# First layer's input projection weights in buffers of their own, loaded once and kept for both chains

## The chip, the cores and the metric

The kernel runs on one core of a Trainium2 chip. The metric is the device time of one execution in microseconds (us): the median of several runs, and beside it the time of the one execution that the profiler recorded. The engines are TensorE (PE in the rows; its weight loads are PEld), VectorE (DVE), ScalarE (ACT), GpSimd (POOL) and SyncE (SP, which only issues transfers). Transfers issued by SP, ACT and POOL run on 16 shared DMA engines.

## What is computed

Two layers of a backbone that runs two groups of tokens through the same weights: 128 context tokens (one block, `b = 0`) and 256 latent tokens (two blocks, `b = 1, 2`). Cut to what matters here:

```
for l in range(2):
    mod = silu(cond) @ w_mod[l] + b_mod[l]          # 6 vectors of 1024; sh1, sc1, g1, sh2, sc2, g2
    h   = LN(x) * (1 + sc1) + sh1
    proj = h @ w_in[l]                              # 1024 x 1696, for context AND latent tokens
    mix = concat(gqa(proj), mla(proj), gmlp(proj)) @ w_o[l]
    x   = LN(alpha * x + g1 * mix)
    h2  = LN(x) * (1 + sc2) + sh2
    q   = h2 @ peer_wq[l];  ids, g = top-k of the product keys of q
    x   = LN(alpha * x + g2 * sum_k g_k * gelu(u[ids_k] . h2) * v[ids_k])   # PEER, 16384 experts
```

The latent tokens attend to cached context keys, not to the context chain's own result, so within a layer the two chains are independent. `w_in[l]` (6.95 MB in float32) is needed by both.

## The kernel before, in words

Each layer has a first stage (projection, attention, output projection of both chains, then the product-key queries of the context) and a second stage (PEER). In PEER the latent tokens go densely over all experts on TensorE, while for the 128 context tokens VectorE works on rows that GpSimd gathers (`gt`, four buffers, 256 gathers a layer: `u_step` and `v_step`). The gathers can start when the context's `ids` are written.

A scheduler decides the order on each engine, from the order in which the code is emitted, from priorities (`hp()` lifts the context chain, `crit()` lifts it further) and from its own timing; each engine then runs its list in order. Large weights come through a ring of six 512 KB buffers (`ring`, `RB = 6`), all issued by SP: a piece's load waits on SP until the piece six places earlier has been used, and everything behind it in SP's list waits too. In the first layer the ring serves `wm` (pieces of `w_mod`, eight to one of the six vectors; `wm_1`, `wm_0` are scale and shift, without which no projection can start), `wic` and `wil` (14 pieces of `w_in` for context and latents, the same data, loaded once for each chain by `project`), `woc`/`wol` (pieces of `w_o`), `wq` (query weights) and later the expert tables.

`project` makes `hT` (normalised, modulated, transposed input), then takes the 14 pieces in turn: eight matmuls per token block into a PSUM bank (`psic` context, `psil` latents), copied out by ScalarE to `proj`. The string `ORD` says in which order the first layer's parts are emitted: `p` the context projection, `2 4 3` three vectors of `w_mod`, `a` attention and `o` output projection of the context, each `l` one piece of the latents' projection. After it come `ctx_picks` (context queries `psqp`, scores `pssk`, `top_list`, `routing` to `ids`), what is left of the latents' projection, five vectors of the second layer's `w_mod`, the latents' attention (`pssl` scores, `psT` transposes, `pso` values) and their output projection (`psol`), then the sixth vector of the first layer. PSUM tag `m` has one bank, shared by `psm` (the sums of `w_mod`), `psc` (their transposes) and the context scores.

Of the kernel before, what the change touches and what calls it, by code (L numbers as in the profile page):

```python
# [8 lines left out]
F32 = mybir.dt.float32  # L9
# [36 lines left out]
def tile_fn(ctx: ExitStack, tc, A, outs):  # L46
    nc = tc.nc
# [5 lines left out]
    def pool(es, name, bufs=1, **kw):  # L53
        return es.enter_context(tc.tile_pool(name=name, bufs=bufs, reuse_waits="tile", **kw))
# [9 lines left out]
    def psum(es, spec):  # L64

        for tag, n in spec.items():
            banks[tag] = pool(es, f"ps_{tag}", n, space=PSUM)

    def pS(tag, name):
        return banks[tag].tile([128, 512], F32, name=name, tag=tag)  # L70

    def run(g, n=None):

        for k, _ in enumerate(g):
            if n is not None and k + 1 == n:
                return

    def hp():
        return tc.high_priority(offset=HP) if HP else ExitStack()

    def crit(on=True):
        return tc.high_priority(offset=2 * HP) if CRIT and on else ExitStack()
# [71 lines left out]
    def load(src, name, n=1024, cring=None):  # L154

        t = ring.tile([128, 1024], F32, name=name, tag="ring") if cring is None else             cring.tile([128, 1024], F32, name=name, tag="cring", bufs=2)
        nc.sync.dma_start(t[:, :n], src)
        return t[:, :n]
# [34 lines left out]
    def transposed_mod(b, l, ks, kh, dst4, name, XP, tag):  # L193

        r = 0 if b == 0 else 1
        xh = XP.tile([128, D], F32, name=name + "xh", tag="xh")
        normalise(xh, x[b], *ln_stats(x[b], name, "clk"[b], xh if b in AL1 else None))
        for h in range(2):
            ps = pS(tag, name + "pst")
            for c in range(4):  # L200
                T.transpose(ps[:, c * 128:(c + 1) * 128], xh[:, (h * 4 + c) * 128:(h * 4 + c + 1) * 128], ident)
            d = dst4(h)
            for c in range(4):
                cc = h * 4 + c
                sc, sh = cols[l][:, ks, cc, r:r + 1], cols[l][:, kh, cc, r:r + 1]
                if c % 2:
                    V.tensor_scalar(d[:, c, :], ps[:, c * 128:(c + 1) * 128], sc, sh, op0=OP.mult, op1=OP.add)
                else:
                    hmark.append(S.activation(d[:, c, :], ps[:, c * 128:(c + 1) * 128], AF.Identity, bias=sh,
                                              scale=sc))  # L210
        return xh
# [35 lines left out]
    def project(l, ch):  # L247

        ch.hT = {b: ch.P.tile([128, 8, 128], F32, name=f"hT{b}", tag=f"hT{i}") for i, b in enumerate(ch.bs)}
        for b in ch.bs:  # L250
            with crit(b):
                transposed_mod(b, l, 1, 0, lambda h: ch.hT[b][:, h * 4:h * 4 + 4, :], "m1", ch.P, ch.tT)
        ch.proj = {b: ch.P.tile([128, IN_W], F32, name=f"proj{b}", tag=f"proj{i}") for i, b in enumerate(ch.bs)}
        for j in range(14):
            w0 = j * 128
            n = min(128, IN_W - w0)
            wv = load(A["w_in"][l, :, w0 * 8:(w0 + n) * 8], f"wi{ch.g}{j}", n * 8, ch.cring)
            wv = wv.rearrange("p (c n) -> p c n", c=8)
            for b in ch.bs:
                ps = pS(ch.tS, "psi" + ch.g)  # L260
                for c in range(8):
                    T.matmul(ps[:, :n], lhsT=ch.hT[b][:, c, :], rhs=wv[:, c, :], start=(c == 0), stop=(c == 7))  # L262
                S.activation(ch.proj[b][:, w0:w0 + n], ps[:, :n], AF.Copy)
            if j == 9 and ch.ctxg:
                p0 = ch.proj[0]
                nc.scalar.dma_start(o_v[0, l].rearrange("s k d -> s (k d)"), p0[:, O_V:O_V + 128])
                nc.scalar.dma_start(o_kr[0, l], p0[:, O_KR:O_KR + 32])
            yield j

    class Chain:  # L270

        def __init__(self, l, bs, P, W, cring=None):
            self.l, self.bs, self.P, self.W, self.cring = l, bs, P, W, cring
# [372 lines left out]
    def out_c(cc):  # L646
        with ExitStack() as e1:
            cc.out_proj(e1)
# [101 lines left out]
    for l in range(DEPTH):  # L750
        last = l + 1 == DEPTH

        with ExitStack() as es3:
            psum(es3, BK[min(l, 1)])
            with ExitStack() as esc:
                Pc = pool(esc, f"cb{l}")
                if l:
                    with hp():
                        ctx_close(l - 1, pk, Pc)
                Pl = pool(es3, f"lp{l}", side="right")  # L760
                Wl = Shared(l, Pc, Pl)
                if l:
                    Wl.load()
                lat = Chain(l, [1, 2], Pl, Wl)
                cc = Chain(l, [0], Pc, Wl, pool(esc, f"cr{l}") if l else None)
                pl_ = project(l, lat)
                def first():
                    run(project(l, cc))
                    if l == 0:
                        with tc.issue_after(hmark[-1].ins):  # L770
                            Wl.load()
                            for t, n in late:
                                nc.scalar.dma_start(t, A[n])

                st_ = {"p": first, "2": lambda: modulation(0, 2, "m"),
                       "4": lambda: modulation(0, 4, "m"), "3": lambda: modulation(0, 3, "m"),
                       "a": lambda: cc.attention_in(esc), "o": lambda: out_c(cc)}
                for k in (ORD if l == 0 else ORD1):
                    if k == "l":
                        run(pl_, 1)  # L780
                    else:
                        with hp():
                            st_[k]()
                with hp():
                    pk = ctx_picks(l, cc, esc)
                run(pl_)
                if not last:
                    mods = [(l + 1, v) for v in (1, 0, 2, 4, 3, 5)]
                    for _ in range(MB):
                        modulation(*mods.pop(0), "m")  # L790
                lat.attention(pool(es3, f"lb{l}", side="right"))
                lat.out_proj()
                if l == 0:
                    modulation(0, 5, "m")

        with ExitStack() as es_:
# [200 lines left out]
            for k, r in RATES[l].items():  # L997
                ms = marks[k]
                n = int(len(ms) * r + 0.5)
# [24 lines left out]
N0 = [50,60]  # L1024
MB = 5
ORD1 = 'paollllllllllllll'
ORD = 'p2ll4ll3llaollllllll'
HP = 100000
KA = 0.375
KO = 0  # L1030
# [92 lines left out]
```

## Time and profile before

| | |
|---|---|
| three runs | 2406.20, 2408.43, 2412.51 us; median 2408.43 |
| profiled execution | 2407.9 us, span 2406.1 us, mean granted TensorE clock 0.972 |
| busy share of the span | PE 94%, DVE 79%, ACT 46%, POOL 29% |
| moved from HBM | 689.14 MB read, 4.16 MB written |

The span is the time from the first to the last instruction; 1.8 us of the profiled execution lie around it. A busy share is an average over stages with different limits. The first layer's first stage lasts to 342 us of the span, where the latents' transposes for PEER (`m2pst`) begin.

### The profile page before, as it was taken

The page shows a single profiled execution, that of the slowest core. Times are in us where ns is not written, and L with a number is a line of the kernel's source. Part 1 is how long each engine was busy: PE and PEld are TensorE (multiplying, and loading weights), DVE is VectorE, ACT ScalarE, POOL GpSimd, SP SyncE. Part 2 cuts the span into 40 slices and gives each one's busy share as a digit, 9 for nine tenths or more (in the row PEclk, how much of TensorE's full clock was granted, in tenths as well). Part 3 has the DMA queues.
Part 4 walks back from the last instruction along what each step waited for, and adds up shares of the span by engine and source line. Part 5 has one row for each costly group of instructions (what it writes and reads, how often), then busy time and mean ns, then how long its engine had stood idle before and what let it go on. Part 6 is the DMA issues. An engine that isn't in the chain of part 4 may idle for free.

```text
span 2406.1 us, 41658 instructions
## 1 busy us (share of the span) xinstructions
PE 2260.6 (94%) x15660; PEld 1914.5 (80%) x15660; DVE 1904.6 (79%) x3942; ACT 1115.2 (46%) x2084; POOL 697.7 (29%) x523
## 2 busy tenths in 40 slices
PE   6999889999999999999989996989999999998997
PEld 5686469999998995667778785889999889855886
DVE  3157579996898888898863468899879888899987
ACT  3324532442785445444445553134348744444444
POOL 0000233454004433464200003435530143344630
PEclk8999989999999999999999998999999999998998
DMA  9967889999658999999863355989985599987994
GB/s 331 322 193 265 336 322 348 324 358 350 219 159 295 360 332 347 328 352 374 299 213 113 120 158 196 325 313 349 363 320 159 188 374 346 333 309 270 395 364 147
DMA packets 196314, 696.05 MB, mean 289 GB/s; under 512 B 22992, under 2 KB 27408, under 8 KB 196112
## 3 DMA queue, kind: packets, MB, share of 16 engines
q1 hardware_dynamic: 110016, 398.52, 46.7%
q0 software_dynamic: 74736, 272.14, 31.1%
q10 hardware_dynamic: 11360, 22.73, 2.8%
q8 instruction: 123, 2.02, 0.3%
q14 instruction: 79, 0.65, 0.1%
HBM read 689.14 MB, written 4.16 MB: 288 GB/s over the span
## 4 chain that ended last, share of the span: by engine, by line
PE 32%; DVE 8%; issue 8%; DMA 2%; POOL 1%; ACT 1%; DVEq 0%; ACTq 0%; POOLq 0%
PE acc L926 18%; PE psA L852 6%; DVE gt L692 2%; PE psil L262 2%; DMA gt<-in_peer_u_dram,ids 1%; POOL gt L686 1%; PE psqp L561 1%; PE psic L262 1%; DVE ulo L847 1%; PE psoc L522 1%; PE pssl L421 1%; DMA wic<-in_w_in_dram 1%; PE psW L890 0%; DVE idx L550 0%; DVE rep L548 0%
## 5 line engine op out<-in xcount | busy, mean ns | idle before, releaser
L686 POOL DMA_INDIRECT gt<-in_peer_u_dram,ids x256 | 325.3, 1271 | 1185.6 <-DVE gt L692 478.4
L686 POOL DMA_INDIRECT gt<-in_peer_v_dram,ids x256 | 368.0, 1438 | 464.0 <-DVE acc L703 434.7
L926 PE MATMUL acc<-vhi,pp 128*128 128x512 f32 x1728 | 441.9, 398 | 15.6 <-ACT pp L906 9.4
L852 PE MATMUL psA<-h2hi,uhi 128*128 128x256 f32 x1664 | 416.2, 287 | 5.1 <-ACT uhi L846 5.1
L852 PE MATMUL psA<-h2lo,uhi 128*128 128x256 f32 x1664 | 411.3, 284 | 0.0
L926 PEld LDWEIGHTS acc<-vhi,pp 128*128 128x128 f32 x1728 | 326.1, 191 | 86.3 <-ACT pp L906 10.0
L915 ACT ACTIVATE vhi<-v 128x1024 fp32r<-128x1024 f32 x216 | 228.7, 1060 | 274.0 <-PE acc L926 161.2
L692 DVE SCALAR_TENSOR_TENSOR gt<-gt,h2c 128x1024 f32<-128x1024 f32 x256 | 309.5, 1216 | 28.0 <-DMA gt<-in_peer_u_dram,ids 27.9
L703 DVE SCALAR_TENSOR_TENSOR acc<-gt,wcol,acc 128x1024 f32<-128x1024 f32 x254 | 325.5, 1282 | 6.2 <-DMA gt<-in_peer_v_dram,ids 5.2
L846 ACT ACTIVATE uhi<-u 128x1024 fp32r<-128x1024 f32 x208 | 220.0, 1058 | 230.2 <-PE psA L852 107.5
L852 PEld LDWEIGHTS psA<-h2hi,uhi 128*128 128x128 f32 x1664 | 319.7, 192 | 7.9 <-ACT uhi L846 5.7
L852 PEld LDWEIGHTS psA<-h2lo,uhi 128*128 128x128 f32 x1664 | 320.0, 192 | 2.1
L847 DVE TENSOR_TENSOR ulo<-u,uhi 128x1024 fp32r<-128x1024 f32 x208 | 254.3, 1223 | 79.9 <-ACT uhi L846 74.7
L916 DVE TENSOR_TENSOR vlo<-v,vhi 128x1024 fp32r<-128x1024 f32 x216 | 263.6, 1223 | 52.6 <-ACT vhi L915 47.7
L852 PE MATMUL psA<-h2hi,ulo 128*128 128x256 f32 x1664 | 239.4, 286 | 1.0 <-DVE ulo L847 0.8
L926 PE MATMUL acc<-vlo,pp 128*128 128x512 f32 x864 | 234.3, 392 | 1.5 <-DVE vlo L916 1.4
L852 PEld LDWEIGHTS psA<-h2hi,ulo 128*128 128x128 f32 x1664 | 216.2, 192 | 3.0 <-DVE ulo L847 1.6
L872 ACT ACTIVATE e<-iota,nid 128x128 f16<-128x128 f16 x512 | 158.9, 426 | 112.1 <-PE psW L890 112.1
L926 PEld LDWEIGHTS acc<-vlo,pp 128*128 128x128 f32 x864 | 162.3, 189 | 35.8 <-DVE vlo L916 2.5
L852 PE MATMUL psA<-h2T,u 128*128 128x256 f32 x768 | 171.8, 379 | 0.0
L852 PEld LDWEIGHTS psA<-h2T,u 128*128 128x128 f32 x768 | 143.1, 190 | 18.1
L926 PE MATMUL acc<-v,AR 128*128 128x512 f32 x320 | 143.6, 599 | 0.0
(437 smaller groups left out, 3039.9 us busy)
## 6 DMA issues: line engine op xcount, KB each, us to landing
u<-in_peer_uT_dram SPq DMA_DIRECT2D x256, 512.0 KB, 6.0
v<-in_peer_v_dram SPq DMA_DIRECT2D x256, 512.0 KB, 6.0
wm<-in_w_mod_dram SPq DMA_DIRECT2D x96, 512.0 KB, 7.2
wq<-in_peer_wq_dram SPq DMA_DIRECT2D x64, 512.0 KB, 4.7
wic<-in_w_in_dram SPq DMA_DIRECT2D x26, 512.0 KB, 5.7
wil<-in_w_in_dram SPq DMA_DIRECT2D x26, 512.0 KB, 4.2
woc<-in_w_o_dram SPq DMA_DIRECT2D x16, 512.0 KB
wol<-in_w_o_dram SPq DMA_DIRECT2D x16, 512.0 KB, 3.6
```

Of the source, the lines that this page charges most:

```text
L262: T.matmul(ps[:, :n], lhsT=ch.hT[b][:, c, :], rhs=wv[:, c, :], start=(c == 0), stop=(c == 7))
L421: T.matmul(sb[i][:, m * nk:(m + 1) * nk], lhsT=lhs(i, h), rhs=rhs(h), start=True, stop=True)
L686: nc.gpsimd.indirect_dma_start(out=t, out_offset=None, in_=tab, in_offset=bass.IndirectOffsetOnAxis(ap=pk.ids[:, j:j + 1], axis=0))
L692: V.scalar_tensor_tensor(t, t, 1.0, pk.h2c, op0=OP.mult, op1=OP.mult, accum_out=acol[:, j:j + 1])
L703: V.scalar_tensor_tensor(pk.acc, t, wcol[:, j:j + 1], pk.acc, op0=OP.mult, op1=OP.add)
L846: S.activation(hi, ua, AF.Copy)
L847: marks["A" if ii < NA else "U" if ii < NA + PRE else "B"].append(V.tensor_sub(lo, ua, hi.bitcast(F32)))
L852: T.matmul(ps[:, a * 256:(a + 1) * 256], lhsT=lw[:, c * 128:(c + 1) * 128], rhs=rw[:, c, :], start=(k == 0), stop=(k == len(passes) - 1))
L872: S.activation(e2[:, t // TI, :, t % TI], iota1, AF.Abs, bias=nb_[:, t0 % 128 + t:t0 % 128 + t + 1])
L915: S.activation(hi, v, AF.Copy)
L916: marks["O" if ii >= NA else "Q" if ii >= NA - PRE else "P"].append(V.tensor_sub(lo, v, hi.bitcast(F32)))
L926: T.matmul(accp[tb][h], lhsT=pl[:, tb * 128:(tb + 1) * 128], rhs=vr[:, h * 512:(h + 1) * 512], start=st0, stop=sp)
```

## The change

In the first layer both chains share a dictionary `kept` and a pool `keep` on the right side of SBUF: 14 tiles, one for each piece of `w_in`. The chain that comes first to a piece (the context's, since `p` is first in `ORD`) issues the load into the piece's own tile; the other finds it there. The pool is closed behind the latents' projection, before the pool of the latents' attention is opened on the same side. `ORD` is also shorter by six `l`, so that six of the latents' 14 pieces are emitted after `ctx_picks` rather than before. The second layer goes the old way.

```diff
@@ project @@
-            wv = load(A["w_in"][l, :, w0 * 8:(w0 + n) * 8], f"wi{ch.g}{j}", n * 8, ch.cring)
+            if ch.kept is not None and j in ch.kept:
+                wv = ch.kept[j]
+            elif ch.kept is not None:
+                wv = ch.kept[j] = ch.keep.tile([128, n * 8], F32, name=f"wi{j}")
+                nc.sync.dma_start(wv, A["w_in"][l, :, w0 * 8:(w0 + n) * 8])
+            else:
+                wv = load(A["w_in"][l, :, w0 * 8:(w0 + n) * 8], f"wi{ch.g}{j}", n * 8, ch.cring)
...
@@ tile_fn @@
+                esk = es3.enter_context(ExitStack())
+                if l == 0:
+                    lat.keep = cc.keep = pool(esk, "keep", side="right")
+                    lat.kept = cc.kept = {}
...
                 run(pl_)
+                esk.close()
...
-ORD = 'p2ll4ll3llaollllllll'
+ORD = 'p2ll4ll3llaoll'
```

The new tiles wait for nothing, so the scheduler puts their loads first of all. In SP's list, at its very start, the pieces of `w_in` (`wi`, 14 of them) now stand ahead of the condition vector `cond` and of `w_mod`, and are gone from behind it (+ is the change):

```order
+L261 DMA wi_301<-in_w_in_dram 128x1024
...
+L261 DMA wi_447<-in_w_in_dram 128x1024
+L261 DMA wi_459<-in_w_in_dram 128x256
 L87 DMA cond<-in_cond_dram 128x16
 L157 DMA wm_10_110<-in_w_mod_dram 128x1024
...
 L157 DMA wm_07_211<-in_w_mod_dram 128x1024
-L157 DMA wic_298<-in_w_in_dram 128x1024
...
-L157 DMA wic_456<-in_w_in_dram 128x256
```

What moved: 14 loads past `cond` and the 16 pieces of `wm_1` and `wm_0`; the latents' 14 loads (`wil`), which stood in five groups farther down among `wm`, `woc` and `wq`, are gone.

On TensorE, where the two chains' projections begin (behind the last piece of `wm_0`), before:

```order
L166 MATMUL psm<-wm_07_211,silu 32x256 x4
L178 MATMUL psc<-ident,modrow 128x128 x2
L262 MATMUL psic<-wic_298,hT_264 128x128 x8
L262 MATMUL psic<-wic_310,hT_264 128x128 x3
L201 MATMUL m1pst<-ident,m1xh 128x128 x8
```

and of the change:

```order
L166 MATMUL psm<-wm_07_211,silu 32x256 x4
L178 MATMUL psc<-ident,modrow 128x128 x2
L166 MATMUL psm<-wm_20_485,silu 32x256 x4
L166 MATMUL psm<-wm_21_491,silu 32x256 x4
L268 MATMUL psil<-wi_301,hT_539 128x128 x2
L166 MATMUL psm<-wm_22_497,silu 32x256 x4
L268 MATMUL psic<-wi_301,hT_267 128x128 x7
```

What moved: two pieces of the next vector stand between the transposes `psc` and the first projection, and from there on `w_mod` and both projections are mixed.

On VectorE, behind the context's `ids` (the gathers' start; `gt` is a gathered row, `modrow` the finished sum of a `w_mod` vector, `pT`, `mx` and `sums` belong to the latents' attention, `y` to their output projection), before:

```order
L676 TENSOR_TENSOR ids<-i_1873,i_1874 128x128
L285 TENSOR_TENSOR rp_2513<-qr,ropeM 128x128
...
L171 TENSOR_TENSOR modrow<-psm,bm 128x256
L443 COPY pT<-psT 128x3x128
L173 TENSOR_SCALAR modrow<-modrow 128x256
...
L427 RECIPROCAL sums<-sums 128x2
L423 TENSOR_REDUCE mx<-pssl 128x1
L692 SCALAR_TENSOR_TENSOR gt,acol<-gt,h2c 128x1024
L443 COPY pT<-psT 128x3x128
```

and of the change:

```order
L684 TENSOR_TENSOR ids<-i_1728,i_1729 128x128
...
L460 COPY mTl<-pso__2745 64x256
L700 SCALAR_TENSOR_TENSOR gt,acol<-gt,h2c 128x1024 x2
L171 TENSOR_TENSOR modrow<-psm,bm 128x256
L700 SCALAR_TENSOR_TENSOR gt,acol<-gt,h2c 128x1024
L173 TENSOR_SCALAR modrow<-modrow 128x256
L181 COPY cols_102<-psc 128x8 x2
L700 SCALAR_TENSOR_TENSOR gt,acol<-gt,h2c 128x1024 x4
L171 TENSOR_TENSOR modrow<-psm,bm 128x256
```

What moved: before, most of the latents' attention stood behind `ids` and one gathered row at a time among it; now the attention is nearly done at `ids`, and seven gathered rows stand ahead of the last `modrow` of the stage, behind which TensorE has its transposes and then `psol`.

## Rows read from the trace of the kernel before

**Rows 1.** The page: busy time (share of the span), and DMA by 40 slices.
```profile
PE 2260.6 (94%) x15660; PEld 1914.5 (80%) x15660; DVE 1904.6 (79%) x3942; ACT 1115.2 (46%) x2084; POOL 697.7 (29%) x523
...
DMA  9967889999658999999863355989985599987994
GB/s 331 322 193 265 336 322 348 324 358 350 219 159 295 360 332 347 328 352 374 299 213 113 120 158 196 325 313 349 363 320 159 188 374 346 333 309 270 395 364 147
```

**Rows 2.** Windows: length, busy us of each engine, PE clock, DMA share, GB/s.
```profile
0.00:34.89 34.89, 16.09 (x149) 6.41 (x149) 9.68 (x32) 11.44 (x25) 1.99 (x7) 0.86 0.97 377
34.89:68.89 34.00, 32.38 (x272) 29.59 (x272) 9.59 (x32) 8.84 (x30) 0.00 (x0) 0.95 0.87 272
68.89:125.07 56.18, 51.63 (x447) 36.47 (x447) 10.26 (x34) 22.71 (x74) 0.00 (x0) 0.97 0.89 318
125.07:163.84 38.77, 36.02 (x297) 34.86 (x297) 25.69 (x64) 8.42 (x30) 0.00 (x0) 0.96 0.63 193
163.84:210.40 46.56, 46.56 (x407) 45.31 (x405) 26.03 (x136) 10.44 (x42) 0.00 (x0) 1.00 0.68 222
210.40:301.71 91.31, 82.13 (x594) 41.26 (x593) 59.82 (x225) 52.27 (x124) 13.02 (x12) 0.98 0.85 321
301.71:342.00 40.29, 32.59 (x301) 28.03 (x301) 32.69 (x76) 8.62 (x20) 17.70 (x15) 0.92 0.83 299
342.00:850.00 508.00, 499.33 (x3762) 468.72 (x3763) 447.48 (x999) 255.07 (x417) 169.10 (x132) 0.99 0.85 304
```

**Rows 3.** Timeline of PE: start, length, what, count, idle before it and its releaser.
```profile
29.98 1.08 PE L166 MATMUL psm<-wm,silu 128*32 128x256 f32 x8 [0.20 <-DMA wm<-in_w_mod_dram]
...
34.89 4.48 PE L262 MATMUL psic<-wic,hT 128*128 128x128 f32 x22 [2.59 <-DVE hT L207]
```

**Rows 4.** The page, DMA issues: count, size, median us to landing.
```profile
wil<-in_w_in_dram SPq DMA_DIRECT2D x26, 512.0 KB, 4.2
...
wil<-in_w_in_dram SPq DMA_DIRECT2D x2, 128.0 KB, 3.3
```

**Rows 5.** The tile `wm` from 0 to 70 us, its last line.
```profile
DMA to landing us min/median/max: 6.4/8.4/10.3
```

**Rows 6.** Waits of PE, 34.9 to 349.2 us: total, times, longest.
```profile
PE psm L166 <- DMA wm<-in_w_mod_dram: 13.8, 12, 2.1
...
PE psic L262 <- DVE hT L207: 2.6, 1, 2.6
PE pso__1068 L450 <- ACT pT L437: 1.9, 1, 1.9
```

**Rows 7.** Timeline of PE, from the context's first score product to its output projection.
```profile
68.07 0.64 PE L166 MATMUL psm<-wm,silu 128*32 128x256 f32 x8 [0.83 <-DMA wm<-in_w_mod_dram]
...
73.44 1.16 PE L421 MATMUL pssc<-kTc,qTc 64*128 64x128 f32 x8
...
80.77 0.44 PE L436 MATMUL psT<-ident,pt 128*128 128x128 f32 x2
...
90.02 0.64 PE L166 MATMUL psm<-wm,silu 128*32 128x256 f32 x8 [1.31 <-DMA wm<-in_w_mod_dram]
...
129.99 4.35 PE L522 MATMUL psoc<-woc,mTc 128*128 128x128 f32 x22 [1.36 <-DVE mTc L452]
...
134.39 3.74 PE L522 MATMUL psoc<-woc,mTc 128*128 128x128 f32 x32
```

**Rows 8.** Timeline of DVE and of POOL, where the gathers start.
```profile
253.84 0.29 DVE L676 TENSOR_TENSOR ids<-i,i 128x128 int32<-128x128 f32 x1
...
254.41 0.99 POOL L686 DMA_INDIRECT gt<-in_peer_u_dram,ids  x1 [251.33 <-DVE ids L676]
...
256.98 0.94 POOL L686 DMA_INDIRECT gt<-in_peer_u_dram,ids  x1 [0.30 <-issue]
```

**Rows 9.** The tile `gt`, 254 to 300 us: its work on DVE, and its landing.
```profile
L692 DVE SCALAR_TENSOR_TENSOR gt<-gt,h2c x8: 1205/1215/1217, 265.8 to 296.4; 128x1024 f32<-128x1024 f32 x8
...
DMA to landing us min/median/max: 4.4/8.2/12.0
```

More of the change, by code (lines that the diff above doesn't have):

```diff
@@ L270, in tile_fn @@
     class Chain:
+        keep = kept = None
         def __init__(self, l, bs, P, W, cring=None):
```

## The prediction

> **What bounds the kernel now.** The page first: TensorE is busy 94% of the span, VectorE 79%, the DMA engines mostly in the tenths 6 to 9 [rows 1]. A mean says little about a change in the first 140 us, so the windows come next, cut at the joints of the first stage [rows 2]. The reader is to see three things. Up to 34.89 us the DMA engines are full (0.97, 377 GB/s) and TensorE works 16.09 us of 34.89: it waits for pieces of `w_mod`, the last at 29.98, then for `hT`, and starts projecting at 34.89 [rows 3]. From there to 301.71, where the latents' output projection runs in one piece, TensorE is busy 248.7 of 266.8 us, so only 18.1 us are idle. Then PEER follows, in which TensorE is busy 499.33 of 508 us. The waits tell what the idle time is: `w_mod` pieces, `hT`, softmax [rows 6]. So the first 30 us belong to the DMA engines, all that follows to TensorE, and what TensorE starts later it can only make up out of those 18 us.
>
> **The change part by part.** The sum is made against the profiled execution, 2407.9 us, 1.8 more than its span; the median, 2408.43, is 0.5 above it. Runs differ by 6 us, so 0.3% (7.2 us) is about what can be told from no change.
>
> *One set of loads goes.* The latents' 13 loads of 512 KB and one of 128 KB in this layer [rows 4] are 13 x 0.524 + 0.131 = 6.95 MB. Spread from 69 to 157 us, they use DMA time where TensorE was busy 92 to 95% [rows 2], so they are worth only the waits that they cause: for `w_mod` pieces before 125 us, 0.83 and 1.31 [rows 7]. The rows show DMA at 0.87 to 0.97 there, but TensorE short of work for 4.5 us of 56 at most. The Trainium skill (Perfetto Trace Analysis, Identifying the Most-Contended Engine) has one optimize the engine with the highest use, for DMA its share of the HBM rate; by that rule dropping 6.95 MB would itself be the gain, and the sum about -18 instead of +16; the trace does not bear this out behind 35 us. The sum goes by the busy TensorE; the other reading is a rival below.
>
> *The other set moves to the front.* In SP's order the 14 loads now stand ahead of `cond` and the 16 pieces of `wm_1` and `wm_0`, without which nothing can be projected. Does an earlier issue hold the later ones back? A `w_mod` piece takes 6.4 to 10.3 us to land, median 8.4, with up to six of 0.524 MB under way [rows 5]; six at 377 GB/s are 8.3 us, so a piece waits for those issued ahead. The 6.95 MB cost 6.95 / 0.377 = **18.4 us** (17.6 at the 395 GB/s of the best slice, 21.0 at the 331 of the first [rows 1]). The last piece of `wm_0` lands at about 48, and the projection starts at 53.3 instead of 34.89. VectorE's and ScalarE's early normalisation hides behind this, but it was hidden before too; nothing else can use the time, since TensorE has only a few transposes of other work.
>
> *What comes back.* Two pieces of `wm_2` now run before the first projection, 2 x 0.64 [rows 7]: **-1.3**. All of `w_in` is then in SBUF, so the latents' projection fills TensorE without waiting for the ring. I take back the waits on `w_mod` above (2.1), the slow run behind the idle stretch at 130 us (22 matmul halves in 4.35 us, where 32 later take 3.74 [rows 7]: 4.35 - 22 x 0.117 = 1.8), about 1 of the wait for `pT` (1.9 [rows 6]) and 1 of small ones: **-6**. The bounds are 0 and the whole 18.1. I stay near the lower third, because 9.2 of the 18.1 lie between 210 and 302, where the latents' attention, five `w_mod` vectors and the gathers meet at 0.85 DMA share [rows 2]; the change leaves them together.
>
> *New waits.* First, the latents' projection used to fill TensorE while the context's output normalisation and queries ran; it is now used up before `psoc`, and the order puts the latents' first heads there, score products directly ahead of their own transposes. A softmax from scores to transposes took 80.77 - 73.44 - 1.16 = 6.2 us [rows 7]; TensorE has one other head's scores to do meanwhile, about another 1.2 us. One such gap at full price is 5.0; part of it goes to the second half of `psoc`: **+3** (0 to 8). Second, the gathers. About half of the latents' attention now precedes the last context query. Of the 82.13 us of TensorE between 210.40 and 301.71, 40 `w_mod` pieces are 25.6 and 16 output matmuls 1.8, which leaves 55, so half is 27. `ids`, at 253.84 before [rows 8], comes at about 253.8 + 18.4 + 27 - 5 = 294. Behind it VectorE's order has seven gathered rows ahead of the stage's last `modrow`, and TensorE's `psol` waits for that. Four buffers: the third gather is issued 2.9 us behind `ids` (1.27 apart [rows 8]), lands 8.2 later, takes 1.2 on VectorE [rows 9] and frees its buffer for the seventh: 2.9 + 8.2 + 1.3, then 0.2 + 8.2 + 1.2 more, 22 us. Behind `ids` TensorE has about 20 us of work left before `psol` by the order (16 `w_mod` pieces, 10 us, and the last three heads' transposes and values, by my count of the order also 10), so this wait shows as **+2** (0 at a landing of 4.4; at 12.0 it is 2 x 3.8 more, +10). Queued behind those gathers are the latents' `y` and normalisation, on which all of PEER hangs.
>
> *Nothing.* The new tiles cost no copy. The shorter `ORD` moves priorities only; what it does is in the orders already counted. From 342 us on, the same matmuls come in nearly the same order, with as many gathers ahead of each mark (within one), and TensorE is 98% busy, so a delay passes through to the end whole. In the second layer's PEER some matmuls change places; I allow 3 us either way.
>
> The sum: 18.4 - 1.3 - 6 + 3 + 2 = +16.1, 2407.9 + 16.1 = **2424**.
>
> **The rivals.** (a) *Everything is made up*: TensorE, with all projection weights at hand, loses almost none of its idle 18.1 us; say 14 come back and no new wait shows. 18.4 - 1.3 - 14 = +3, 2411: no difference that counts. For it: a filler that never waits. Against it: half of the idle time lies behind 210 us, where no filler was missing.
>
> (b) *Fewer bytes win* (the other side). If the first stage is bound by what the DMA engines move, 6.95 MB less at 377 GB/s end it 18.4 us sooner: 2389.5. For it: DMA share 0.87 to 0.97 up to 125 us [rows 2]. Against it: TensorE's 248.7 busy us still have to follow the first projection, so even without any idle time it ends at 53.3 + 248.7 - 1.3 = 300.7, against 301.71. Even with no idle time left it takes 7.2 us off only if the first projection starts before 301.7 - 7.2 - 247.4 = 47 us, that is, if the leading loads hold `w_mod` back by less than 12 us.
>
> (c) *The gathers hold the stage*: each lands in 12.0 us, as the slowest did [rows 9], since `w_mod` and `w_o` pieces land at the same time. The gather wait becomes +10 and little is given back: 18.4 - 1.3 - 3 + 3 + 10 = +27, 2435. For it: the order leaves nothing to do behind the gathers. Against it: fewer pieces of other data are under way by then.
>
> (d) *No change in the loads' effect*: a kept tile could still be loaded twice or wait for the ring. The order excludes both: 14 loads, none with a place in the ring.
>
> **How the numbers follow.** The forecast, 2416 to 2431, has 0.62; (c) 0.15, (a) 0.16, (b) 0.07. Slower by over 0.3%: 0.62 + 0.15 = 0.77; the same: 0.16; faster: 0.07. The bounds of the terms by themselves reach from -2 (17.6 - 1.3 - 18.1) to +38 (21.0 - 1.3 + 8 + 10); for 8 in 10 the range takes in (a) and (c) but not (b) or those ends: 2411 to 2436.
>
> **What the profile would show.** TensorE's first projection at 53 us, not 35 (16 pieces of `w_mod` landing between 20 and 48); DMA full until then and well below 0.8 from 60 to 160; no wait of TensorE for `w_in`, nearly none for `w_mod` before 200; `ids` near 294; VectorE waiting for a gather's landing just behind it, which it hardly did before; `m2pst` near 358 instead of 342; the same distance from there to the end. The prediction is wrong if the first projection starts before 47 us, if idle time of TensorE from there to `psol` is under 8 us, or if PEER takes up the delay.

## The result, and the profile after

The changed kernel takes 2439.73 us (median of 4 runs, 2438.84 to 2440.55) against 2410.47 for the kernel before on the same chip (4 runs, 2406.2 to 2416.2): ratio 1.0123, 95% interval 1.0106 to 1.0139, slower by 1.2%. The forecast was slower too, but 2424, with a range of 2411 to 2436. The profiled executions stand 32.7 us apart in span (2438.8 and 2406.1), the medians 29.3.

The page after: busy time and share, and the DMA engines by 40 slices of 61 us [rows 1].
```profile
PE 2271.7 (93%) x15660; PEld 1922.0 (79%) x15660; DVE 1898.5 (78%) x3937; ACT 1121.4 (46%) x2092; POOL 685.5 (28%) x523
...
DMA  9624899999756999989964344999995599987994
GB/s 385 224 72 130 326 366 351 325 351 350 275 157 221 370 340 339 340 296 388 359 214 142 117 156 162 323 329 339 344 326 176 160 379 344 350 300 266 390 365 154
```
Slices 2 to 4 moved 224, 72 and 130 GB/s, where before they moved 322, 193 and 265. The windows of the first stage, cut at its new joints, answer to [rows 2]: length, busy us of each engine, PE clock, DMA share, GB/s.
```profile
0.00:51.56 51.56, 23.00 (x164) 8.38 (x164) 9.33 (x31) 11.08 (x24) 1.99 (x7) 0.94 0.99 388
51.56:161.11 109.55, 106.72 (x952) 92.53 (x948) 20.03 (x75) 33.25 (x114) 0.00 (x0) 1.00 0.44 157
161.11:200.53 39.42, 34.44 (x190) 24.37 (x189) 28.77 (x90) 24.09 (x54) 0.00 (x0) 0.83 0.45 150
200.53:253.90 53.37, 51.43 (x369) 43.07 (x368) 31.36 (x140) 24.00 (x80) 0.00 (x0) 1.00 0.50 158
253.90:303.00 49.10, 45.70 (x393) 23.81 (x394) 35.82 (x161) 26.30 (x62) 4.59 (x5) 1.00 0.93 347
303.00:326.40 23.40, 9.95 (x77) 2.58 (x77) 9.69 (x18) 0.00 (x0) 5.79 (x7) 0.62 1.03 409
326.40:369.06 42.66, 36.01 (x321) 31.45 (x321) 33.93 (x82) 7.57 (x19) 18.44 (x16) 0.90 0.93 345
369.06:877.00 507.94, 496.46 (x3736) 465.39 (x3737) 443.29 (x993) 254.02 (x415) 161.64 (x130) 0.99 0.84 301
```
The DMA engines are half idle from 51.56 to 253.9 (0.44 to 0.50) and full from there to 369 (0.93 to 1.03). TensorE is busy in 87 to 97% of each window up to 303. The sixth line is the place to look at: 9.95 us of work in 23.4, on a granted clock of 0.62. TensorE's timeline shows the start [rows 3] and that place:
```profile
51.56 1.12 PE L268 MATMUL psil<-wi,hT 128*128 128x128 f32 x4
...
53.18 1.05 PE L268 MATMUL psic<-wi,hT 128*128 128x128 f32 x7
...
307.45 0.66 PE L178 MATMUL psc<-ident,modrow 128*128 128x128 f32 x2 [3.82 <-DVE modrow L173]
...
313.62 0.64 PE L166 MATMUL psm<-wm,silu 128*32 128x256 f32 x8 [1.63 <-DMA wm<-in_w_mod_dram]
316.17 1.08 PE L166 MATMUL psm<-wm,silu 128*32 128x256 f32 x8 [1.91 <-DMA wm<-in_w_mod_dram]
318.74 1.08 PE L166 MATMUL psm<-wm,silu 128*32 128x256 f32 x8 [1.49 <-DMA wm<-in_w_mod_dram]
...
326.40 1.01 PE L530 MATMUL psol<-wol,mTl 128*128 128x128 f32 x3 [0.25 <-DMA wol<-in_w_o_dram]
```
From 313 on a `w_mod` piece arrives every 2.55 us, and TensorE does nothing else till 325. What shares the DMA engines with it is seen on VectorE and GpSimd [rows 8]:
```profile
292.00 0.29 DVE L684 TENSOR_TENSOR ids<-i,i 128x128 int32<-128x128 f32 x1
...
300.74 1.23 DVE L700 SCALAR_TENSOR_TENSOR gt<-gt,h2c 128x1024 f32<-128x1024 f32 x1 [4.88 <-DMA gt<-in_peer_u_dram,ids]
...
304.81 0.94 POOL L694 DMA_INDIRECT gt<-in_peer_u_dram,ids  x1 [1.62 <-DVE gt L700]
307.36 0.93 POOL L694 DMA_INDIRECT gt<-in_peer_u_dram,ids  x1 [1.62 <-DVE modrow L173]
...
324.99 0.42 DVE L171 TENSOR_TENSOR modrow<-psm,bm 128x256 f32<-128x256 f32 x1 [7.20 <-PE psm L166]
```
Gathers are issued 2.6 to 2.9 us apart. The last line is the stage's last `modrow`: it waits 7.20 us for TensorE's sum, not for a gathered row; the seventh row was done at 317.8. They land in 8.0, 9.3 and 12.0 us (the tile `gt` from 291 to 330, least, median, most), which answers to [rows 9]. The DMA view of 303 to 326.4 us (packets, MB, share of 16 engines by queue; q1 holds SP's loads, q0 the gathers) shows the two in nearly equal parts:
```profile
q1 hardware_dynamic: 1359, 4.94, 52.8%
q0 software_dynamic: 1235, 4.47, 47.9%
```

### The profile page after: what moved, and what is told of

It is laid out like the page before. It is cut to its first block, busy times and chain, and to the rows that moved or that the text cites. A ratio compares the mean times of both kernels' runs of the same rounds, so it can differ in the third digit from the quotient of the medians.

```text
span 2438.8 us, 41594 instructions
## 1 busy us (share of the span) xinstructions
PE 2271.7 (93%) x15660; PEld 1922.0 (79%) x15660; DVE 1898.5 (78%) x3937; ACT 1121.4 (46%) x2092; POOL 685.5 (28%) x523
## 4 chain that ended last, share of the span: by engine, by line
PE 44%; issue 8%; DVE 5%; DMA 5%; POOL 4%; ACT 1%; DVEq 0%; POOLq 0%; ACTq 0%
PE acc L939 19%; PE psA L865 16%; POOL gt L694 4%; DMA gt<-in_peer_v_dram,ids 3%; PE psil L268 2%; DMA gt<-in_peer_u_dram,ids 1%; PE psqp L569 1%; DVE gt L700 1%; PE psW L903 1%; PE psoc L530 1%; PE psic L268 1%; PE pssl L429 1%; DMA wic<-in_w_in_dram 0%; DMA lnr<-in_lnp_dram 0%; PE psT L450 0%
## 5 line engine op out<-in xcount | busy, mean ns | idle before, releaser
L694 POOL DMA_INDIRECT gt<-in_peer_u_dram,ids x256 | 315.8, 1234 | 1229.5 <-DVE gt L700 481.8
L711 DVE SCALAR_TENSOR_TENSOR acc<-gt,wcol,acc 128x1024 f32<-128x1024 f32 x254 | 325.5, 1282 | 14.9 <-DMA gt<-in_peer_v_dram,ids 13.8
L700 DVE SCALAR_TENSOR_TENSOR gt<-gt,h2c 128x1024 f32<-128x1024 f32 x256 | 308.7, 1216 | 33.8 <-DMA gt<-in_peer_u_dram,ids 33.5
L865 PEld LDWEIGHTS psA<-h2lo,uhi 128*128 128x128 f32 x1664 | 321.5, 193 | 2.1
```

What stands on the lines that cost most here:

```text
L694: nc.gpsimd.indirect_dma_start(out=t, out_offset=None, in_=tab, in_offset=bass.IndirectOffsetOnAxis(ap=pk.ids[:, j:j + 1], axis=0))
L700: V.scalar_tensor_tensor(t, t, 1.0, pk.h2c, op0=OP.mult, op1=OP.mult, accum_out=acol[:, j:j + 1])
L711: V.scalar_tensor_tensor(pk.acc, t, wcol[:, j:j + 1], pk.acc, op0=OP.mult, op1=OP.add)
L865: T.matmul(ps[:, a * 256:(a + 1) * 256], lhsT=lw[:, c * 128:(c + 1) * 128], rhs=rw[:, c, :], start=(k == 0), stop=(k == len(passes) - 1))
```

## The experiments

All are compared with the kernel before by the ratio of runs on one chip. Of each edit the lines that do it are shown; lists that only collect handles are left out. The table has the landmarks in each trace, us: the first projection product, `ids`, the start of the first and of the last `psol` product of the first layer's latents, the second `m2pst` row of the latents. (The expectation of e20 has 354.8 for the last `psol` of the change; that is a row of several products.) In some runs a few `psol` products run ahead of the rest: before, 20 of 256 stand ahead of 301.7. The profiled executions of e2, e7, e15 and e20 took 6 to 9 us more than the medians of their runs.

| run | start | ids | psol first | last | m2pst | median | ratio, 95% |
|---|---|---|---|---|---|---|---|
| before | 34.9 | 253.8 | 294.3 | 329.6 | 347.4 | 2410.5 | 1 |
| the change | 51.6 | 292.0 | 326.4 | 357.7 | 375.1 | 2439.7 | 1.0106 to 1.0139 |
| e1_hold | 45.5 | 293.1 | 327.9 | 359.7 | 380.0 | 2443.7 | 1.0102 to 1.0151 |
| e1b_hold | 34.5 | 291.9 | 327.0 | 358.4 | 378.6 | 2443.3 | 1.0128 to 1.0164 |
| e14_one | 39.6 | 281.9 | 321.5 | 354.5 | 373.3 | 2443.2 | 1.0096 to 1.0157 |
| e2_gathers | 51.5 | 293.6 | 320.2 | 357.5 | 378.2 | 2443.9 | 1.0099 to 1.0148 |
| e3_early | 51.8 | 302.6 | 309.1 | 346.4 | 366.3 | 2431.6 | 1.0063 to 1.0107 |
| e12_bytes | 51.7 | 293.0 | 306.7 | 343.5 | 362.4 | 2426.7 | 1.0039 to 1.0086 |
| e4_ord | 36.7 | 239.8 | 315.5 | 345.6 | 363.2 | 2428.7 | 1.0040 to 1.0086 |
| e13_bef_bytes | 35.3 | 251.1 | 323.4 | 368.0 | 385.0 | 2451.6 | 1.0149 to 1.0202 |
| e15_bef_early | 35.6 | 258.5 | 295.2 | 334.2 | 354.5 | 2418.5 | 1.0018 to 1.0045 |
| e7_ctx | 52.1 | 297.0 | 332.0 | 363.6 | 381.0 | 2443.9 | 1.0114 to 1.0153 |
| e8_ctx_hold | 36.4 | 297.8 | 336.7 | 369.2 | 386.8 | 2443.6 | 1.0129 to 1.0173 |
| e10_all | 35.8 | 286.4 | 307.8 | 348.1 | 368.2 | 2432.5 | 1.0071 to 1.0116 |
| e16_held | 51.5 | 296.1 | 322.9 | 356.3 | 372.7 | 2458.6 | 1.0189 to 1.0223 |
| e17_bef_held | 35.3 | 254.2 | 293.8 | 332.0 | 349.1 | 2448.1 | 1.0135 to 1.0183 |
| e18_one_held | 37.9 | 280.2 | 308.1 | 343.5 | 360.4 | 2452.9 | 1.0156 to 1.0195 |
| e19_early_held | 51.5 | 302.2 | 308.7 | 346.8 | 363.8 | 2457.1 | 1.0173 to 1.0213 |
| e20_order | 52.3 | 266.6 | 340.8 | 380.2 | 400.4 | 2458.9 | 1.0169 to 1.0218 |
| e21_order_one | 38.5 | 255.6 | 318.9 | 358.2 | 378.6 | 2451.7 | 1.0126 to 1.0180 |

### The late start

**e1_hold**: the kept loads behind `wm_0` in SP's order (`dm` are the ring's loads in order; 15 is the last of `wm_0`).
```diff
+                with tc.issue_after(dm[15].ins):
                     nc.sync.dma_start(wv, A["w_in"][l, :, w0 * 8:(w0 + n) * 8])
```


> The change, but SP issues the 14 kept loads behind the last of the 16 pieces of wm_1 and wm_0, not ahead of cond. Theory A (the late start and, apart from it, a full DMA at the end of the stage): the first projection starts near 35 us instead of 51.6, and the kernel ends about 17 us earlier than the change, 2422 to 2425, still 12 to 15 slower than before, since w_mod pieces and gathers still meet ahead of the latents' output projection. Theory B (TensorE runs out of independent work once the latents' projection is used up, and that costs the rest): the same start, but the stalls grow, since the projection is used up earlier still: 2430 or more. Theory C (the start is all that matters): 2410, as before.

Measured: no gain. The first projection came at 45.53, behind a wait of 12.13 us for `hT`: ScalarE's order has the load of `wm_2`'s bias row (`bm`) ahead of it, and that issue stood till 44. **e1b_hold** adds an edge that puts this load behind `hT` (`after` is the context's `hT` for `wm_2`, and nothing for the other vectors).
```diff
-        nc.scalar.dma_start(bm, A["b_mod"][l, v])
+        with tc.issue_after(after.ins) if after is not None else ExitStack():
+            nc.scalar.dma_start(bm, A["b_mod"][l, v])
```


> As the run in which SP issues the kept loads behind wm_1 and wm_0, and ScalarE issues the load of wm_2's bias row behind the hT it has to write (in that run hT stood behind this issue and the first projection waited 12.1 us for it, till 45.5). Theory D (the ring in its order): from 254 us on the DMA engines are full up to the latents' queries, and that stretch begins when the context's queries free the ring of the wq pieces; the kernel ends earlier by about what the context's queries start earlier. First projection near 35 us, context's queries 10 to 16 us earlier than in the change (207.9), end 2424 to 2430. Theory E (TensorE's own sum: only its start and idle time count): 2423. Theory F (the start does not matter at all, as the run with the start at 45.5 us and no gain would have it): 2438 to 2442.

Measured: the projection starts at 34.5, and nothing is gained. ScalarE's rows show why the start is not a real one: `bm` is issued at 47.34, and the row behind it waits.
```profile
47.34 0.34 ACTq L171 DMA_DIRECT2D bm<-in_b_mod_dram  x1
47.73 0.46 ACT L211 ACTIVATE hT<-m1pst,cols 128x128 f32<-128x128 f32 x1 [12.24 <-DMA wi<-in_w_in_dram]
```
The issues that follow it on ScalarE's queue (`gain`, `w_ukv`, `wsT`, `bsT`, `w_uq`) stand 1 to 4 us apart till 56.7, and TensorE worked 14.29 us from 30 to 60, where the change worked 24.14. In front or behind, 7 MB at once hold up somebody: `w_mod` there, ScalarE's small loads here. So these two runs can't tell what an early start is worth. **e14_one** loads only one of the kept tiles:
```diff
-            if ch.kept is not None and j in ch.kept:
-                wv = ch.kept[j]
+            if ch.kept:
+                wv = ch.kept[0][:, :n * 8]
```


> The change with only the first of the kept tiles loaded, and used for all 14 projection steps of both chains: the other 13 loads (6.4 MB), and with them the right projection, are left out; nothing then stands ahead of w_mod but 0.5 MB. First projection at 36 to 37 us. Theory E: the whole late start is given back, 2422 to 2424. Theory D: the context's queries come earlier by as much and the full DMA stretch with them, 2422 to 2428. Theory F (the late start does not matter, since what follows waits for something else): 2436 to 2442.

Measured: 12 us earlier at the start are 10 at `ids`, 5 at the first `psol`, 3 at the last, 2 at `m2pst`, and none at the end. The gain went into waits for `w_mod` (waits of PE, 282 to 374 us):
```profile
PE psm L166 <- DMA wm<-in_w_mod_dram: 18.9, 11, 3.1
```
against 13.7 us in 11 waits in the change from 292 to 376. Theories D and E both asked for 2428 or less; theory F had the right end. The late start is real, but in this order of work it is not what the end hangs on.

### The bytes behind the context's queries

**e2_gathers** (`om[8]`: the first of the latents' `y` products):
```diff
+                if l == 0 and j < 12:
+                    with tc.issue_after(om[8].ins):
+                        f()
```


> The change, but VectorE takes the context's first 12 gathered rows only behind the first product of the latents' output projection, so that just four gathers (as many as there are buffers) transfer ahead of it. Theory A: the last wait of psc for modrow (3.8 us) goes and the last eight w_mod pieces come about 1.4 instead of 2.6 us apart, 8 to 10 us less up to there; seven rows are then done later on VectorE, which PEER has to take up: 2430 to 2434. Theory B: the gathers are not what holds the stage, 2438 to 2441. A third possibility, that the gathers pace the stage after it: 2440 to 2450.

Measured: from `ids` to the first `psol` 26.6 us instead of 34.4, the 8 that theory A asked for; but the last `psol` and the end stay. With four gathers ahead of `psol` instead of eleven, nearly all that the DMA engines carry in front of it are weight loads, and still TensorE waits. TensorE's timeline, the window of the last eight pieces, and its DMA queues:
```profile
307.35 1.08 PE L167 MATMUL psm<-wm,silu 128*32 128x256 f32 x8 [0.60 <-DMA wm<-in_w_mod_dram]
...
315.14 1.08 PE L167 MATMUL psm<-wm,silu 128*32 128x256 f32 x8 [0.20 <-DMA wm<-in_w_mod_dram]
316.41 1.08 PE L167 MATMUL psm<-wm,silu 128*32 128x256 f32 x8 [0.19 <-DMA wm<-in_w_mod_dram]
317.70 1.08 PE L167 MATMUL psm<-wm,silu 128*32 128x256 f32 x8 [0.21 <-DMA wm<-in_w_mod_dram]
```
```profile
307.35:318.80 11.45, 8.64 (x64) 1.61 (x64) 0.00 (x0) 0.00 (x0) 0.00 (x0) 0.50 1.03 408
```
```profile
q1 hardware_dynamic: 1226, 4.45, 97.6%
...
q0 software_dynamic: 20, 0.06, 1.3%
```
A piece now comes every 1.28 us. The rows held back transfer beside the `wm_5` pieces, which come 2.55 us apart in their turn (358.56 to 368.73): the bytes were moved, not saved.

**e3_early** moves two vectors (`m` runs the next `modulation(1, v)`), with `MB = 3`:
```diff
-ORD = 'p2ll4ll3llaoll'
+ORD = 'p2ll4ll3llmamoll'
```


> The change, but two of the five w_mod vectors of the second layer that stood behind the context's queries (16 of 40 pieces, 8.4 MB) are put among the latents' projection, where the DMA engines moved 23 GB/s. TensorE's work is the same. Theory A: DMA share there rises from 0.08 to about 0.5, the last w_mod pieces ahead of the latents' output projection come without waiting, and 9 to 13 us come back: 2427 to 2431. Theory B expects a gain too, but in the softmax waits between 160 and 200 us (5 us idle and 3 in slow matmuls), and the waits for w_mod at 303 to 326 us stay: 2431 to 2435. If neither holds, 2440.

Measured: 2431.6, a gain of 8. Windows of this run:
```profile
100.00:157.00 57.00, 57.00 (x513) 46.11 (x506) 8.64 (x32) 17.63 (x61) 0.00 (x0) 1.00 0.56 200
...
302.00:342.00 40.00, 37.50 (x294) 31.68 (x291) 27.61 (x69) 9.38 (x22) 16.17 (x17) 1.00 0.95 347
```
The idle DMA time at 100 to 157 us is used, and TensorE works 37.50 of the 40 us in which the change worked 25.84. `ids` came 10 us later, and still `psol` started 17 earlier.

**e12_bytes**, and **e13_bef_bytes** with the same edit on the kernel before:
```diff
-            w = load(A["w_mod"][l, v, c], f"wm{l}_{v}{c}")
+            if c == 0 or l == 0 or bank != "m":
+                w = load(A["w_mod"][l, v, c], f"wm{l}_{v}{c}")
```


> The change, but the five w_mod vectors of the second layer that stand behind the context's queries load one piece each and use it for all eight of their products: 35 loads of 0.524 MB (18.4 MB) are left out, and with them the right values of these vectors; TensorE's products are as many as before. Theory D (between the context's queries and the latents' queries the DMA engines, full from 254 to 375 us, set the end): the waits of 1.4 to 1.9 us for pieces at 308 to 326 and 361 to 366 us go, the second normalisation transpose for PEER comes 15 to 25 us earlier than at 375.1, and the kernel ends at 2415 to 2425. Theory E (TensorE's own sum, the late start of 17 us above all): at most 8 us, 2432 to 2440.

> The same 35 loads left out of the kernel before. Theory D: there the same bytes are spread over 137 us at 318 GB/s and TensorE is busy nearly throughout, so they cost little more than the waits for w_mod: 3 to 10 us, 2400 to 2407, clearly less than the change gains from it. Theory E: about as much as the change gains from it.

Measured, e12: TensorE's products are the same and 18.4 MB less are loaded; the last `psol` comes 14 us earlier and the kernel ends 13 earlier, a little short of theory D's range. e13 went the other way, 40 us slower than before, which no theory had. There 54 gathers were issued ahead of the second `m2pst`, where before there were 26 and in the change 27: the built order of VectorE has 31 gathered rows ahead of the last maximum of the latents' scores (`mx`), where before there are 6 and in the change none. The waits of 210 to 390 us:
```profile
DVE gt L693 <- DMA gt<-in_peer_u_dram,ids: 23.5, 22, 3.2
...
PE pso__2511 L451 <- DVE pT L444: 7.0, 1, 7.0
PE psqmT L222 <- ACT qm L408: 6.1, 2, 3.8
PE psmx L222 <- DVE oc L485: 5.4, 1, 5.4
```
VectorE stands in its order at gathers that haven't landed, and TensorE waits for `pT` and `oc` behind them. So e12 against e13 doesn't tell what the bytes alone are worth in the kernel before; that stays open.

### The order

**e4_ord**: the kernel before with the change's `ORD`, nothing else.
```diff
-ORD = 'p2ll4ll3llaollllllll'
+ORD = 'p2ll4ll3llaoll'
```


> The kernel before with the shorter order string alone (the last six projection steps of the latents are emitted behind the context's queries), w_in still loaded twice through the ring. All theories, and the prediction, cost this at nothing: 2407 to 2414, the same as before. If the string alone costs more than 7 us, part of the loss belongs to it and not to the kept weights.

Measured: 2428.7, 15 us slower by the ratio, from a string that the prediction costed at nothing. `ids` comes 14 earlier, the latents' first score product 17 later (225.0 against 208.3), the last `psol` 16 later, with 13 gathered rows ahead of the latents' last `mx` (6 before). With kept weights the string does nothing: the change built with the old string (built, not run) has the same order on every engine, buffer numbers apart. So the loss is not the string's, but it shows what the order at this place is worth.

**e7_ctx** (`pm[-1]`: the last `psic` product) and **e8_ctx_hold**, e7 and e1b together:
```diff
+                    with tc.issue_after(pm[-1].ins) if pm and l == 0 and not ch.ctxg else ExitStack():
```


> The change, but TensorE takes the latents' projection products only behind the last of the context's (psil behind psic, as it was before the change); the kept loads stand ahead of everything as in the change. TensorE's work and the loads' bytes are the same. Theory D: psic takes some 36 instead of 46 us, the context's queries start 8 to 12 us earlier, and the kernel ends that much earlier: 2428 to 2432. Theories E and F: 2438 to 2442.

> Both of these together: kept loads and bias row behind wm_0 and hT, and psil behind psic. Theory D: first projection near 35 us, psic done near 72, the context's queries near 180 and no later than in the kernel before plus 16; end 2408 to 2418. Theory E: 2423. Theory F: 2438 to 2442.

Measured: neither gains. In e7 `psic` still takes 43 us, since TensorE has 17 `w_mod` pieces to do between (before, four or five in 35 us), and the context's queries start at 212.4, later than the change's 207.9. In e8 they start at 200.9, 7 us earlier than in the change, but the last `psol` comes 11.5 later, and the end is that of the change. Theory D as it stood there (the context's queries set the end) falls with these two. **e10_all** is e8 and e3:

> These together, and two of the five w_mod vectors of the second layer ahead of the context's queries, among the latents' projection, where the change left the DMA engines idle. Theory D: the full DMA stretch ahead of the latents' queries loses 8.4 MB, which brought 8 us by itself: 2400 to 2410. Theory E: 2423, for TensorE's work is the same. If the context's queries are held up by the moved pieces (10 us of TensorE), nothing is gained against the run without them.

Measured: 2432.5, what e3 gives by itself. **e15_bef_early** moves one vector in the kernel before (`ORD = 'p2ll4ll3llamollllllll'`, `MB = 4`):

> The kernel before, w_in through the ring twice, with one of the five w_mod vectors of the second layer moved ahead of the context's queries, where the DMA share was 0.65. Theory D: the stretch behind the queries is lighter by 4.2 MB; the waits for w_mod at 332 to 342 us (7 us) shrink, but the context's queries come 5 us later: 2402 to 2411. Theory E: no change, 2407 to 2413.

Measured: 0.32% slower. There 35 gathers were issued ahead of the second `m2pst` (before, 26), and 8 rows stand ahead of the last `mx`.

**e20_order** and **e21_order_one** (`qm[47]`: the last product of `psoc`'s sixth chunk), the second with e14's single tile:
```diff
+                    mk = None if l or ch.ctxg else pm[-1] if j < 6 else qm[47]
+                    with tc.issue_after(mk.ins) if mk is not None else ExitStack():
```


> The change with TensorE's order of before: the latents' projection products of steps 0 to 5 queue behind the last psic, those of steps 6 to 13 behind the sixth chunk of psoc, so that they run beside the context's queries again and not ahead of them; loads, bytes and TensorE's work are those of the change. Theory I (what costs is that kept weights let the whole latents' projection and half of the latents' attention run ahead of the context's queries, so that ids, the w_mod pieces and the gathers come 38 to 44 us later and are pressed into the time that is left): ids near 265 to 275 instead of 292, last psol near 340 to 345 instead of 354.8, end 2422 to 2430, the late start alone. If the order is not it: 2437 to 2443.

> The same order with one kept tile loaded and used for all 14 steps (13 loads and the right projection left out), so that the projection starts near 38 us. Theory I: ids near 255 to 260, the end 2408 to 2416, 10 to 14 us ahead of the run with all loads: with the order of before an earlier start is worth its whole length. If the start does not matter in this order either, both runs end within 4 us.

Measured: `ids` comes early as wanted, but both lose. What was put back is the projection's place, not the order of before as a whole: the latents' scores now start at 250 (208 before). TensorE's timeline of e20:
```profile
237.89 0.66 PE L179 MATMUL psc<-ident,modrow 128*128 128x128 f32 x2 [6.59 <-DVE tv L609]
...
253.41 0.91 PE L434 MATMUL pssl<-kTl,qTl 64*128 64x384 f32 x2 [1.38 <-DVE cols L182]
```
`modrow` stands behind the context's top-list on VectorE. Besides, 20 gathered rows stand ahead of the latents' last `mx` in e20 and 14 in e21 (none in the change); what they cost was not tried. Theory I is not shown by this. The start 13.8 us earlier is worth 22 us at the last `psol` and 9.9 at the end (by the ratios, with 8.8 of uncertainty): not nothing here, as in e14.

### The gathers out of the way

**e16_held** (`gm[3]`: the last `h2lo`), **e17_bef_held** the same before, **e18_one_held** on e14, **e19_early_held** on e3:
```diff
+                if l == 0 and j < 50:
+                    with tc.issue_after(gm[3].ins):
+                        f()
```


> The change, with VectorE taking all of the context's gathered rows only behind the last h2lo of the latents' queries; of the 27 gathers that ran ahead of them only four (as many as there are buffers) still do, so 12 MB leave that stretch. Theory H (from the first gather at 292 us to the latents' queries at 375 the DMA engines, at 375 GB/s, set the pace, a gather and a weight piece in turn, and neither TensorE's start nor its order matters): the second m2pst comes at 348 to 358 instead of 375.1, w_mod pieces 1.3 instead of 2.55 us apart. The 23 rows are then done in PEER, 28 us of VectorE, which is busy 98% from 400 to 500: if PEER absorbs them, 2412 to 2422; if VectorE holds TensorE there, 2425 to 2445. Theory E (TensorE's sum): m2pst at 368 or later.

> The same hold in the kernel before, where 26 gathers ran from 254 to 347 us beside 76 us of TensorE's work and the DMA share was 0.89. Theory H: less is to be had, the waits for w_mod at 332 to 341 us and part of the last for m2xh: second m2pst at 335 to 341 instead of 347.4; the end 2402 to 2412, or up to 2430 if VectorE in PEER holds TensorE. Theory E: 347 and 2410.

> The change with one kept tile loaded and used for all 14 steps (13 loads and the right projection left out), which started the projection 12 us earlier and gained nothing, now with the rows held back as well. Theory H: with the gathers out of the way the earlier start is worth something again: the second m2pst comes 8 to 12 us earlier than in the run with the hold alone. If it comes at the same time, the weight pieces alone set the stretch, and the start still does not matter.

> The change with two w_mod vectors moved ahead of the context's queries, and the rows held back: 20 MB of 31 leave the stretch from ids to the latents' queries. Theory H: TensorE then sets the pace there; its second m2pst comes at 345 to 355, and the end is that of the hold alone or up to 8 us better. It says whether the two remedies add.

Measured: all four lose 10 to 38 us against the same kernel with its gathers. In e16 the first `m2pst` comes 9 us earlier (359.6), but the second only 2, behind a wait of 12 for the last normalisation; then TensorE loses in PEER (timeline and windows):
```profile
372.68 1.97 PE L202 MATMUL m2pst<-ident,m2xh 128*128 128x128 f32 x8 [12.02 <-ACT m2xh L150]
```
```profile
400.00:500.00 100.00, 92.94 (x561) 85.40 (x560) 99.65 (x432) 31.33 (x48) 37.17 (x35) 0.98 0.93 331
...
650.00:850.00 200.00, 185.40 (x1724) 175.70 (x1723) 183.21 (x290) 131.77 (x242) 59.76 (x42) 0.95 0.73 255
```
In the same windows of the change TensorE worked 96.78 and 196.42 us; VectorE was nearly full in the first of them there too (97.98). The gathers ahead of PEER are worth their place. e18 against e16 is the useful pair: with the gathers gone a start 13.6 us earlier is 12.8 at the last `psol` and 12.3 at `m2pst`, as theory H asked, and 6 at the end. No version beats the kernel before.

## Why the prediction was wrong

*The late start* was sized nearly rightly: the first projection product came at 51.56 and the context's first at 53.18, for a forecast of 53.3, with the DMA engines at 0.99 and 388 GB/s. Its price was not: "a delay passes through to the end whole" holds only while TensorE sets the pace. e14 gives 12 us of it back and the end doesn't move; e18 and e21 get part of it at the end once something else is moved.

*What comes back, and the new softmax waits* (-1.3, -6, +3): from 51.56 to 303 TensorE is idle for 2.83 + 4.98 + 1.94 + 3.40 = 13.2 us of the windows above, against 18.1 in the whole stretch before: 4.9 less, where -6 + 3 asked for 3. By the last score product the change is 0.8 us behind (291.5 against 290.7); but it then has 16 `w_mod` pieces left to do, where before one was left.

*The gathers, "+2 (0 to 10)"*, is the step that failed. `ids` came at 292.0 (294 forecast), seven rows stood ahead of the last `modrow`, a landing took 8 to 12 us, and 16 `w_mod` pieces were left behind `ids`: all as read. The last `modrow` did not wait for the rows, though, but for `psm` (7.20 us). The step counted these 16 pieces as "10 us" of TensorE's work that covers the gathers. They were loads, and they shared the DMA engines with the gathers. The last eight took from 308.49 to 324.92, 16.4 us instead of 8 x 0.64 = 5.1; with the 3.8 us of `psc` behind the rows that is 15.1 instead of 2. e2 tells two parts apart: there the eight pieces took 11.4 us (307.35 to 318.78) and `psc` waited 0.97. So about 8 of the 15.1 are what the gathers took from the loads, and most of the rest is that a piece's own load, at 1.28 us, is twice as long as TensorE's work on it. The price was looked for on VectorE, and stood on TensorE's own filler. Rival (c) came nearest (2435), by luck: landings took 9.3 us in the median and not its 12.0, and its case against itself, "fewer pieces of other data are under way by then", was the very point that was wrong: the DMA share there was 1.03.

*The sum.* At the first `m2pst` (342.00 and 369.06) the change is 27.1 behind, 11.0 more than the +16.1: from first `psic` to `psol` (301.71 before, 326.40 now) it took 273.2 us instead of the forecast 264.5 (+8.7), and from `psol` on 42.7 instead of 40.3 (+2.4). The 2.4 is no longer wait: the waits for `wm_5` pieces shrank from 7.2 to 4.5 us. It is 20 of the 256 output products (2.3 us), which before ran ahead of 301.71. PE's timeline before, then its waits from `psol` to `m2pst`, before and after:
```profile
294.26 1.28 PE L522 MATMUL psol<-wol,mTl 128*128 128x128 f32 x10
...
295.60 1.28 PE L522 MATMUL psol<-wol,mTl 128*128 128x128 f32 x10
```
```profile
PE psm L166 <- DMA wm<-in_w_mod_dram: 7.2, 4, 2.1
```
```profile
PE psm L166 <- DMA wm<-in_w_mod_dram: 4.5, 4, 1.7
```
So the 11.0 arose ahead of `psol`: 13.1 from the gathers' term, less the 1.9 of idle time that came back beyond the forecast, which is 11.2. From the first `m2pst` to the end of the span it is 5.6 more, where I had allowed 3; of these 3.4 are the distance of the two profiled executions from their medians (0.8 above, 2.6 below).

*Is it the bytes?* e12 says so for the change: without 18.4 MB of pieces 13 us are gone. What is left against before, 15.2, is near the 14.1 that the forecast gives without its gather term; that may be chance, since e14 gives its largest term, the start, no price of its own. e3 says it with all loads in place: 8.4 MB earlier, 8 us. The Trainium skill (Perfetto Trace Analysis, Identifying the Most-Contended Engine) was weighed in the prediction as a rule by which fewer bytes win. The kernel moved 6.95 MB less and lost; the bytes went out of a stretch in which the DMA share then fell to 0.08 (100 to 157 us). The same page says, under Optimization Strategy, that where the contended engine changes over time interleaving the regimes may help. e3 agrees with it, and the kernel before, in which the ring paced `w_in` and `w_mod` beside the projection, was that interleaving.

*What stays open.* The late start and the DMA stretch aren't shares of a sum: taking out the first alone gives 0, the second alone 13 of 29, and both together were not run; the other 16 of the 29 were given back by no run. Why the built order puts between 0 (the change) and 31 (e13) gathered rows ahead of the latents' last softmax was not tried; that TensorE waits behind them is shown for e13 only. e16 to e19 change where PEER's rows stand, so their ends say little about the first stage.

## What to carry to other kernels

A filler is cover only if its own loads are there: before counting a matmul as work that hides a wait, look at what the DMA engines carry in that window, gathers included. Dropping a second load saves little where no engine waits for it, and a burst of kept loads takes its time from whatever is queued with it, here on its own queue or on ScalarE's. A delay at the front should be followed from joint to joint, not added to the end, and with an order that a scheduler builds every edit, a string of priorities too, is an edit of the order (15 us here).

## What the runs showed of the hardware

Gathers and weight loads shared the DMA engines in nearly equal parts: 4.47 and 4.94 MB in 23.4 us, one of each about every 2.55 us at 409 GB/s together, although one comes from GpSimd's queue and the other from SP's. The Trainium skill (DMA: Bandwidth & Descriptors, Queues, rings and completion order) says that each DMA engine goes round its queues in turn, a packet at a time; these rows agree. Without gathers beside them (e2) the same pieces came 1.28 us apart, at 408 GB/s.

Of TensorE's clock: with a piece every 2.55 us the granted clock of 303 to 326.4 was 0.62, and rows of eight products took 1.08 us (the lower level, 1.2 GHz) instead of 0.64, so that a piece in the stall cost 0.44 us more of TensorE's time as well. With a piece every 1.28 us (e2) it was 0.50.

A load issued on ScalarE's queue (`bm`, e1b) went out only when, by the profile, loads of SP's queue had landed, and ScalarE stood idle for 12.2 us ahead of the `hT` behind it, although the two have no data in common. This is the program's wait and not the chip's: as built, `bm` waits for a completion semaphore that loads of both queues count up.
